# GLA value weights: differences taken by GpSimd a unit ahead from a second load, instead of by VectorE with a store and a reload

## The chip, the cores and the metric

One core of a Trainium2 chip runs the whole layer as one program. The metric is the device time in microseconds, the median of three runs; lower is better. In the text PE is TensorE (PEld its weight loads), DVE is VectorE, ACT is ScalarE, POOL is GpSimd and SP is SyncE, whose queue issues most DMAs.

## The reference

One decoder layer on 256 tokens of width 2048, in float32. Only the parts that the change touches in full:

```python
proj = x @ w_in                       # (256, 2048) @ (2048, 13336)
gq, gk, gv, gr, glr, fq, fk, fv, ff, ma, mb = jnp.split(proj, offsets, axis=-1)
# branch A: gated linear attention, 4 heads, dk 256, dv 512, diagonal decay
q = gq * DK ** -0.5; k = gk; v = gv
log_a = log_sigmoid(glr @ w_gla_lr + b_gla_lr) / TAU          # TAU = 16
o = gla_chunked(q, k, v, log_a)       # S_t = diag(a_t) S_{t-1} + k_t^T v_t, o_t = q_t S_t
o = rms_norm(o) * silu(gr); y_gla = o @ w_branch_gla
# branch B: softmax attention with forget gates, 8 heads of 128 -> y_fox
merged = sigmoid(ma) * y_gla + sigmoid(mb) * y_fox
x = layer_norm(ALPHA * x + merged @ w_out)
g = causal_dwconv(x @ w_gate); x = layer_norm(ALPHA * x + (gelu(g) * (x @ w_up)) @ w_down)
x = x + sigmoid(x @ w_ple_gate) * (p @ w_ple_proj)
```

`gv` is the product of x with a 2048 x 2048 slice of `w_in`. It is the stage that the change rebuilds.

## The kernel before

**Numbers.** Each float32 weight w is split into hi (w rounded to fp32r, by ACT, L146) and lo = w - hi (by DVE). A product is three fp32r matmuls: x_hi w_hi, x_hi w_lo, x_lo w_hi.

**Units.** All weights pass through as units of 128 x 2048 floats (1 MB), numbered in order of use. `unit()` keeps preparation three units ahead: `prep` issues the loads on SP's queue, in the order of the code, and records ACT's rounding and DVE's subtraction. `raw` (5 buffers), `hi` (6) and `lo` (6) are rings; larger tiles (8 KB a partition) come from a pool of 15 (`s8`). A scheduler orders the instructions of DVE, ACT and PE; SP's order is that of the code.

**Strassen units.** `gv`, `gr`, the output projection, the down projection and the last gate are computed by `s_half` in two column halves of 1024. In each half some of the 8 (or 22) row pairs are multiplied with seven products (`strassen`, 21 matmuls of 512 columns), the others with eight (`classic`, 24). GV is units 56 to 71, GR 72 to 87. `GV_S` names the pairs that take seven products: 11 of the 16 units. A Strassen unit holds the blocks b11, b12, b22, b21 of its weights. Its products need b11, b22, b21 and four differences, called t1 to t4: b12 - b11, b12 - b22 (together `t13`) and b22 - b11, b21 - (b22 - b11) (together `t24`). `prep_s` therefore makes four splits a unit: b11 (512 columns), b2 (1024), t13 (1024) and t24 (1024).

**Where the differences come from, before.** Eight of the 11 units are parked (`GV_T`). At a place of an earlier stage (`PARK_AT`) `park_load` loads the unit, and two places later `park_store` takes the differences on DVE (L203 for 1024 columns, L185 twice for 512) and stores them to DRAM (`td`) by a DMA from POOL's queue (L208). `prep_s` then loads b11 and b2 from the weights and reads t13 and t24 back from `td`. The other three units take their differences in `prep_s` on DVE (L185, four of 512 columns). GR's units are parked in the same way, and stay so.

**The GLA levels.** `a_gen` builds, for two pairs of heads, the decay-weighted attention inside the chunks level by level (1 to 8): DVE and ACT make exponentials and scaled q and k, PE multiplies them in fp32 (L767), and DVE copies the part under a mask into `at` (L772). Level 0 is a column sum with a matrix of ones (L728).

**The lines that the prediction names.** L146 is ACT's rounding; L185 and L203 the differences; L254 the splits in `prep_s`; L286 the split of an ordinary unit; L879 and L1012 add gv's products, and L992 a gate's, out of PSUM; L351 and L353 are matmuls of the stages ahead, L849 those of `s_half`; L341 casts the masks and L1438 copies two columns of the convolution, both on POOL; L521 is one subtraction near the start; L1061 a power on a single column, on POOL.

Of the kernel before, what the change touches and what calls it, by code (L numbers as in the profile page):

```python
# [9 lines left out]
F32 = mybir.dt.float32  # L10
# [14 lines left out]
H = 4  # L25
# [26 lines left out]
T_OG = (1, 2, 1, 1, 1, 2, 1, 1, 0, 2, 1, 1, 0, 1, 1, 3)  # L52
T_AF = (1, 1, 0, 1, 1, 1, 1, 1, 1, 1, 0, 1, 1, 1, 1, 1, 1, 0, 0, 1, 2, 1, 1, 2, 0, 2, 2, 3, 1, 1, 2, 2, 1, 1, 1, 1, 1, 1, 1, 3)
T_X2 = (2, 0, 3, 3, 1, 1)
T_MT = (2, 2, 1, 1, 0, 1, 0, 3, 0, 1, 1, 1, 1, 0, 1, 1)
WO_AT = (2, 0, 6, 1)
WO_P = (8, 0, 5)
WO_STAT = 2
DN_Z = (2, 2)
DN_AT = (3, 8, 3)  # L60
DN_P = (12, 12, 11)
XS_AT = 18
PARK_MA = (1, 5, 10)
PARK_BR = (1, 2, 7, 9)


GV_ORDER = ((1, 0, 4, 2, 3, 5, 7, 6), (1, 4, 6, 3, 2, 0, 5, 7))
GR_ORDER = ((4, 0, 3, 5, 1, 2, 7, 6), (4, 0, 6, 1, 3, 7, 2, 5))
OUT_ORDER = ((4, 5, 1, 0, 2, 3, 6, 7), (2, 0, 5, 3, 1, 6, 4, 7))
# [9 lines left out]
DN_ORDER = ((0, 1, 8, 4, 5, 3, 2, 6, 7, 9, 10, 11, 12, 15, 13, 14, 16, 17, 19, 20, 18, 21), (1, 0, 2, 5, 3, 4, 7, 9, 6, 11, 8, 15, 13, 10, 12, 14, 21, 16, 17, 19, 20, 18))  # L79
DN_S = ((1, 2, 3, 5, 7, 8, 9, 11, 13, 14, 15, 17, 19), (1, 2, 3, 5, 7, 9, 10, 11, 13, 15, 17, 19))  # L80


WO_T = ((0, 1, 2, 5), (1, 3, 5))
# [3 lines left out]
RES_N = (1, 1, 1, 4)  # L87
# [18 lines left out]
def tile_block(ctx: ExitStack, tc: tile.TileContext, wu, wfv, wpp, xT_in, x_in, pT_in, wlr,  # L106
# [48 lines left out]
    for _ in range(8):  # L155
# [17 lines left out]
              for nh in range(2) for n in tset[nh]}  # L173
    parked = {u: i for i, u in enumerate(sorted(parked))}
    td = dr.tile([len(parked), P, 2048], F32, name="td")
    sd = dr.tile([len(DN_U), P, 1024], F32, name="sd")
    hS = {}

# [19 lines left out]
    def park_store(u, w, pinned=False):  # L198
# [8 lines left out]
        differences(w[:, 0:1024], w[:, 1024:2048], 1)  # L207
        nc.gpsimd.dma_start(td[parked[u]], w)  # L208

    def park_plan(units, spots, gap=2):  # L210


        units = [u for u in parked if u in units]
        assert len(units) == len(spots), (len(units), len(spots))
        loaded = {}

        def step(n):
            for u, s in zip(units, spots):
                if s + gap == n:
                    park_store(u, loaded.pop(u), True)  # L220
            for u, s in zip(units, spots):
                if s == n:
                    loaded[u] = park_load(u)

        return step

    def prep_s(u):
# [28 lines left out]

        x11, = split(b11, "b11", slice(512, 1024))
        x22, x21 = split(r1, "b2")
        if u not in parked:
            differences(r0, r1, 0)  # L260
        t1_, t3 = split(rt[0], "t13")
        if u not in parked:
# [4 lines left out]
    def prep(pinned=False):  # L267
        u = n_prep[0]
        n_prep[0] += 1
        if u in s_units:  # L270
            prep_s(u)
            return
        his, los = [], []
        for h in range(2):
            raw = ring.tile([P, 1024], F32, tag="raw", bufs=5, name=f"raw{u}_{h}")
            nc.sync.dma_start(raw, wu[u, :, h * 1024:(h + 1) * 1024])
            hi = rhi.tile([P, 1024], F32R, tag="hi", name=f"hi{u}_{h}")
            copy(hi, raw)
# [7 lines left out]
            i = nc.vector.tensor_tensor(lo, raw, hi.bitcast(F32), ALU.subtract)  # L286
# [419 lines left out]
    at_all = at_gnb[:, 0:1536].rearrange("p (h n) -> p h n", h=H)  # L706
    gnb = at_gnb[:, 1536:2048]

    def a_gen():
        tc.keep_in_program_order(nc.gpsimd.memset(at_all, 0.0))  # L710
        for h in range(H):
            at[h] = at_all[:, h, :]
        for h in range(0, H, 2):
            hs = slice(h, h + 2)
            q, k, b = gq[:, hs, :], gk[:, hs, :], gb[:, hs, :]
# [11 lines left out]
            for i in range(2):  # L727
                nc.tensor.matmul(pa, lhsT=ones, rhs=phl[i].rearrange("p t n -> p (t n)"),  # L728
                                 start=i == 0, stop=i == 1)
            for i in range(2):  # L730
                nc.vector.copy_predicated(A[:, i, 0:256], mask[:, 0, :],
                                          pa[:, i * 256:i * 256 + 256])
            for lev in range(1, 9):
                L = 1 << lev
                h2 = L // 2
                if lev < 8:
# [17 lines left out]
                else:  # L754
                    w4 = lambda x, t: x[:, :, t * 256:t * 256 + 256].rearrange(
                        "p h (c n) -> p h c n", c=2)
                    for t, m in ((0, w4(b, 0)[:, :, :, 127:128]), (1, gt[:, hs, :, :])):
                        nc.vector.tensor_tensor(w4(e, t), w4(b, t),
                                                m.broadcast_to([P, 2, 2, P]), ALU.subtract)
                    nc.scalar.activation(e, e, AF.Exp, bias=0.0, scale=-1.0 / TAU)  # L760
                    nc.vector.tensor_tensor(km, k[:, :, 0:256], e[:, :, 0:256], ALU.mult)
                    nc.vector.tensor_tensor(qm, q[:, :, 256:512], e[:, :, 256:512], ALU.mult)
                yield
# [4 lines left out]
                                         rhs=qm[:, i, c * P:c * P + P], start=c == 0, stop=c == 1)  # L768
                pa = pa[:, 0:256].rearrange("p (h n) -> p h n", h=2)
                if lev < 8:  # L770
                    for i in range(2):
                        nc.vector.copy_predicated(  # L772
                            A[:, i, 0:256].rearrange("p (t n) -> p t n", t=2),
                            mask[:, lev, :].rearrange("p (t n) -> p t n", t=2),
                            pa[:, i:i + 1, :].broadcast_to([P, 2, P]))
                else:
                    copy(A[:, :, 256:384], pa)

# [1022 lines left out]
```

## Time and profile before

| | before |
|---|---|
| median of three runs | 1647.15 us (1645.95 to 1647.29) |
| profiled execution | 1646.94 us, its span 1644.9 us, granted clock 1.0 |
| busy, share of the span | PE 100%, DVE 82%, ACT 58%, POOL 6% |
| DMA | 470.47 MB, mean 286 GB/s |

The span runs from the first to the last instruction; about 2 us lie around it. A row of a group names line, engine, operation and tiles, then "busy us, mean ns of one | idle before it and what ended it". A row of a timeline gives start, length, then the instruction. A row of stretches gives for each engine the busy time in that stretch and the number of instructions.

### The profile page before, as it was taken

How to read it: one execution, taken by the hardware profiler on the slowest of the kernel's cores; microseconds unless marked ns; L12 is line 12 of the kernel's file. 1: busy time of each engine (PE TensorE's matmuls, PEld its weight loads, DVE VectorE, ACT ScalarE, POOL GpSimd, SP SyncE). 2: the span in 40 equal slices, each digit the busy share in tenths (PEclk: the TensorE clock that was granted, in tenths of full speed). 3: DMA queues.
4: the chain of work that ended last, by engine and by line, in shares of the span. 5: the costliest groups of instructions: out<-in, count | busy, mean ns of one | idle time of the engine just before them, and what ended most of it. 6: DMA issues, size and time to landing. Idle time of an engine off the chain costs nothing.

```text
span 1644.9 us, 23447 instructions
## 1 busy us (share of the span) xinstructions
PE 1637.0 (100%) x8407; PEld 1401.3 (85%) x8407; DVE 1355.3 (82%) x1884; ACT 946.2 (58%) x1328; POOL 104.9 (6%) x244
## 2 busy tenths in 40 slices
PE   9999999999999999999999999999999999999998
PEld 9988888888888888888898888888888888888887
DVE  7587799888988975788977888797777788988998
ACT  6654555446666664456575555555555556556655
POOL 0100000000000000000010211121111100000000
PEclk9999999999999999999999999999999999999999
DMA  8789877777877777788857889997877688999575
GB/s 325 267 297 355 295 256 257 259 272 255 323 288 275 253 270 264 272 291 318 298 192 246 283 316 350 342 365 257 277 288 287 222 299 322 348 355 339 206 267 192
DMA packets 115733, 470.47 MB, mean 286 GB/s; under 512 B 13160, under 2 KB 14448, under 8 KB 98720
## 3 DMA queue, kind: packets, MB, share of 16 engines
q1 hardware_dynamic: 106368, 413.38, 71.3%
q0 software_dynamic: 9248, 55.59, 8.4%
q8 instruction: 66, 1.08, 0.2%
q14 instruction: 51, 0.42, 0.1%
HBM read 413.33 MB, written 55.58 MB: 285 GB/s over the span
## 4 chain that ended last, share of the span: by engine, by line
PE 91%; DVE 4%; issue 2%; DMA 2%; ACT 1%; POOL 0%; ACTq 0%; SPq 0%; DVEq 0%; POOLq 0%
PE psm L974 11%; PE psu L351 10%; PE psg L351 9%; PE dn L849 7%; PE psa L974 5%; PE psu L353 5%; PE psg L353 5%; PE gr L849 3%; PE gv L849 3%; PE dn_p L849 3%; PE fv L498 3%; PE psb L974 3%; PE pg L397 2%; PE gv_p L849 2%; PE wo L849 2%
## 5 line engine op out<-in xcount | busy, mean ns | idle before, releaser
L286 DVE TENSOR_TENSOR lo<-raw,hi 128x1024 fp32r<-128x1024 f32 x450 | 546.0, 1221 | 149.3 <-ACT hi L146 147.4
L146 ACT ACTIVATE hi<-raw 128x1024 fp32r<-128x1024 f32 x450 | 473.4, 1058 | 334.1 <-PE psg L351 92.5
L351 PE MATMUL psu<-x1T,hi 128*128 128x512 f32 x688 | 240.4, 392 | 0.0
L351 PE MATMUL psg<-x1T,hi 128*128 128x512 f32 x672 | 234.8, 392 | 0.0
L353 PE MATMUL psu<-x1T,lo 128*128 128x256 f32 x688 | 192.3, 280 | 0.0
L353 PE MATMUL psg<-x1T,lo 128*128 128x256 f32 x672 | 187.8, 280 | 0.0
L974 PE MATMUL psm<-hi,xT 128*128 128x512 f32 x512 | 162.4, 391 | 0.0
L351 PEld LDWEIGHTS psu<-x1T,hi 128*128 128x128 f32 x688 | 129.2, 188 | 27.6
L351 PEld LDWEIGHTS psg<-x1T,hi 128*128 128x128 f32 x672 | 126.2, 188 | 27.0
L146 ACT ACTIVATE hi_b<-raw 128x512 fp32r<-128x512 f32 x118 | 97.9, 842 | 74.3 <-DMA raw<-in_wu_dram 24.0
L254 DVE TENSOR_TENSOR lo_b<-raw,hi_b 128x512 fp32r<-128x512 f32 x118 | 111.0, 954 | 24.6 <-ACT hi_b L146 24.4
L353 PEld LDWEIGHTS psu<-x1T,lo 128*128 128x128 f32 x688 | 130.6, 190 | 0.0
L353 PEld LDWEIGHTS psg<-x1T,lo 128*128 128x128 f32 x672 | 127.6, 190 | 0.0
L974 PEld LDWEIGHTS psm<-hi,xT 128*128 128x128 f32 x512 | 96.2, 188 | 19.6
L254 DVE TENSOR_TENSOR lo_t<-td,hi_t 128x1024 fp32r<-128x1024 f32 x82 | 97.0, 1220 | 6.7 <-ACT hi_t L146 6.5
L974 PE MATMUL psm<-lo,xT 128*128 128x512 f32 x256 | 99.7, 389 | 0.0
L146 ACT ACTIVATE hi_t<-td 128x1024 fp32r<-128x1024 f32 x82 | 84.0, 1055 | 23.2 <-DMA td<-td 11.8
L849 PE MATMUL dn<-hi,hC 128*128 128x512 f32 x304 | 84.9, 389 | 0.0
L974 PE MATMUL psa<-hi,oT 128*128 128x512 f32 x256 | 80.7, 392 | 0.0
L146 ACT ACTIVATE hi_t<-raw 128x1024 fp32r<-128x1024 f32 x36 | 38.2, 1061 | 53.4 <-DVE raw L185 46.8
L849 PEld LDWEIGHTS dn<-hi,hC 128*128 128x128 f32 x304 | 57.0, 188 | 11.8
L1438 POOL COPY gp<-gp 128x1 f32<-128x1 f32 x88 | 43.1, 522 | 276.1 <-DVE gp L380 276.1
(400 smaller groups left out, 3284.5 us busy)
## 6 DMA issues: line engine op xcount, KB each, us to landing
raw<-in_wu_dram SPq DMA_DIRECT2D x527, 512.0 KB, 5.9
td<-in_wu_dram SPq DMA_DIRECT2D x41, 1024.0 KB, 8.8
td<-td POOLq DMA_DIRECT2D x41, 1024.0 KB, 7.5
td<-td SPq DMA_DIRECT2D x41, 1024.0 KB, 8.1
hS<-sd SPq DMA_DIRECT2D x25, 512.0 KB, 7.4
raw<-in_wu_dram SPq DMA_DIRECT2D x41, 256.0 KB, 6.3
sd<-hs POOLq DMA_DIRECT2D x28, 256.0 KB, 6.2
fvraw<-in_wfv_dram SPq DMA_DIRECT2D x13, 524.0 KB, 6.6
```

The source lines that it names most:

```text
L146: return nc.scalar.activation(o, i, AF.Copy, bias=0.0, scale=scale)
L254: nc.vector.tensor_tensor(lo, src, hi.bitcast(F32), ALU.subtract)
L286: i = nc.vector.tensor_tensor(lo, raw, hi.bitcast(F32), ALU.subtract)
L351: nc.tensor.matmul(ps, lhsT=hi[i // 8 if hoff == 0 else 0][:, w0 % 1024:w0 % 1024 + P], rhs=a[:, kt % 4, :], start=first and i == 0, stop= ...
L353: nc.tensor.matmul(ps[:, 256:512], lhsT=lo[i // 8 if hoff == 0 else 0][:, w0 % 1024:w0 % 1024 + P], rhs=a[:, kt % 4, 0:256], start=False, ...
L397: nc.tensor.matmul(bs[j][:, 0:m], lhsT=x, rhs=v[:, o:o + m], start=first and i == 0, stop=last and i == 2)
L498: nc.tensor.matmul(fbk[t][c][:, 0:n], lhsT=x, rhs=w[:, o:o + n], start=kt == 0 and i == 0, stop=kt == 15 and i == 2)
L849: nc.tensor.matmul(ps, lhsT=x, rhs=w, start=todo[id(ps)] == total[id(ps)], stop=todo[id(ps)] == 1)
L974: nc.tensor.matmul(ps, lhsT=x, rhs=v, start=first and i == 0, stop=last and i == 2)
L1438: nc.gpsimd.tensor_copy(g[:, 258 + i:259 + i], g[:, 129 - i:130 - i])
```

## The change

1. `GV_T` is empty: no GV unit is parked. `PARK_AT` has the eight places of GR's units alone.
2. `near` names all 11 GV Strassen units. When `prep` comes to unit u, `near_load` is first called for u and u + 1 (`NEAR_AT = 1`), where not yet done: it loads the whole unit a second time into an `s8` tile (`nw`) on SP's queue and takes the differences in place on POOL, one subtraction of 1024 columns and two of 512. `prep_s` then loads b11 and b2 as for a parked unit and reads t13 and t24 from that tile. Nothing of it is stored.
3. In the GLA levels, level 1 is computed like level 0: a product of neighbouring q and k, one exponential, and a sum by ones in fp32r, instead of four fp32 matmuls per pair of heads. Level 8 has its reference subtracted as ACT's bias, in eight short instructions a pair instead of one long one behind two DVE subtractions. The masked copies take both heads in one instruction.
4. Tables of places and orders of other stages differ (`T_OG`, `T_MT`, `WO_AT`, `OUT_ORDER`, `WO_S`, `DN_ORDER` and others); the numbers of Strassen and parked units in those stages stay.

```diff
-PARK_AT = (1, 4, 5, 8, 13, 13, 14, 17, 22, 24, 29, 34, 37, 43, 43, 47)
+PARK_AT = (4, 8, 13, 18, 24, 32, 40, 47)
-WO_S = ((0, 1, 2, 3, 5), (1, 3, 5))
+WO_S = ((0, 1, 2, 3, 5), (0, 1, 3))
...
-GV_T = ((3, 4, 5), (2, 3, 4, 5, 6))
+GV_T = ((), ())
+NEAR_AT = 1
+GV_N = GV_S
...
+    def near_load(u):
+        w = s8([P, 2048], name=f"nw{u}")
+        nc.sync.dma_start(w, wu[u])
+        o, b, p = [w.rearrange(f, b=2, n=512) for f in (
+            "p (a b n) -> p a b n", "p (a b n) -> p b a n", "p (a b n) -> p a b n")]
+        sub = lambda o, a, b: nc.gpsimd.tensor_tensor(o, a, b, ALU.subtract)
+        sub(o[:, 0], p[:, 0, 1:2].broadcast_to([P, 2, 512]), b[:, 0])
+        b11, b12, b22, b21 = [w[:, 512 * i:512 * i + 512] for i in range(4)]
+        sub(b22, b22, b11)
+        sub(b21, b21, b22)
+        nearw[u] = w
...
-        if u in parked:
+        if u in nearw:
+            nc.sync.dma_start(b11, wu[u, :, 0:512])
+            nc.sync.dma_start(r1, wu[u, :, 1024:2048])
+            w = nearw.pop(u)
+            rt = (w[:, 0:1024], w[:, 1024:2048])
+        elif u in parked:
...
+        for v in range(u, min(NU, u + NEAR_AT + 1)):
+            if v in near and v not in near_done:
+                near_done.add(v)
+                near_load(v)
...
-            for lev in range(1, 9):
+            E, Z = ke[:, 1024:1536], ke[:, 0:512]
...
+            pa = mxtile(f"pa{h}_1")
             for i in range(2):
+                nc.tensor.matmul(pa[:, 0:256], lhsT=ones, rhs=phl[i], start=i == 0, stop=i == 1)
...
+            for lev in range(2, 9):
...
-                    nc.scalar.activation(e, e, AF.Exp, bias=0.0, scale=-1.0 / TAU)
+                    for i in range(2):
+                        for c in range(2):
+                            for t in range(2):
+                                o = t * 256 + c * P
+                                nc.scalar.activation(e[:, i, o:o + P], b[:, i, o:o + P], AF.Exp,
+                                                     bias=gref[:, t, h + i, c:c + 1],
+                                                     scale=-1.0 / TAU)
```

How this moves the instructions, at three places. The names carry the unit's number (`raw59`, `nw60`) and a buffer's; line numbers are those of each kernel. First POOL's order between the GLA levels and the first power of the attention's norm (`gst`), before:

```order
L208 DMA td_106<-td12_2922 128x2048
L208 DMA td_106<-td13_3210 128x2048
L208 DMA td_106<-td14_3212 128x2048
L208 DMA td_106<-td15_3417 128x2048
L1061 ISA
L1061 TENSOR_TENSOR gst_5281<-gst_5281,mhalf_119 128x1
```

And the same place now (the rows go on in this way to `nw70`, then `gst`):

```order
L214 DMA td_106<-td6_3026 128x2048
L214 DMA td_106<-td7_3364 128x2048
L223 ISA
L223 TENSOR_TENSOR nw56_3621<-nw56_3621 128x1024
L223 TENSOR_TENSOR nw56_3621<-nw56_3621 128x512 x2
L223 TENSOR_TENSOR nw58_3732<-nw58_3732 128x1024
L223 TENSOR_TENSOR nw58_3732<-nw58_3732 128x512 x2
L223 TENSOR_TENSOR nw59_3783<-nw59_3783 128x1024
L223 TENSOR_TENSOR nw59_3783<-nw59_3783 128x512 x2
```

POOL has lost eight stores ahead of this place and has 33 subtractions in it. Second, DVE's order at units 59 and 60 of the GV stage, before (59 was not parked, 60 was):

```order
L254 TENSOR_TENSOR lo59_b11_3878<-raw59_0_3873,hi59_b11_3877 128x512
L185 TENSOR_TENSOR raw59_0_3873<-raw59_0_3873 128x512
L185 TENSOR_TENSOR raw59_0_3873<-raw59_0_3873,raw59_1_3874 128x512
L254 TENSOR_TENSOR lo59_b2_3882<-raw59_1_3874,hi59_b2_3881 128x1024
L254 TENSOR_TENSOR lo59_t13_3888<-raw59_0_3873,hi59_t13_3887 128x1024
L185 TENSOR_TENSOR raw59_1_3874<-raw59_1_3874,raw59_0_3873 128x512
L185 TENSOR_TENSOR raw59_1_3874<-raw59_1_3874 128x512
L254 TENSOR_TENSOR lo59_t24_3894<-raw59_1_3874,hi59_t24_3893 128x1024
L254 TENSOR_TENSOR lo60_b11_3928<-raw60_0_3921,hi60_b11_3927 128x512
```

And now:

```order
L279 TENSOR_TENSOR lo59_b11_3843<-raw59_0_3838,hi59_b11_3842 128x512
L279 TENSOR_TENSOR lo59_b2_3847<-raw59_1_3839,hi59_b2_3846 128x1024
L279 TENSOR_TENSOR lo59_t13_3851<-nw59_3783,hi59_t13_3850 128x1024
L279 TENSOR_TENSOR lo59_t24_3855<-nw59_3783,hi59_t24_3854 128x1024
L279 TENSOR_TENSOR lo60_b11_3892<-raw60_0_3887,hi60_b11_3891 128x512
```

The four differences of unit 59 are gone from DVE's order; the four splits of every unit stay. Third, SP's order of loads at the same units, before:

```order
L235 DMA raw58_0_3826<-in_wu_dram 128x512
L236 DMA raw58_1_3827<-in_wu_dram 128x1024
L238 DMA td58_3830<-td_106 128x2048
L242 DMA raw59_0_3873<-in_wu_dram 128x1024
L242 DMA raw59_1_3874<-in_wu_dram 128x1024
L235 DMA raw60_0_3921<-in_wu_dram 128x512
L236 DMA raw60_1_3922<-in_wu_dram 128x1024
L238 DMA td60_3925<-td_106 128x2048
```

And now:

```order
L220 DMA nw59_3783<-in_wu_dram 128x2048
L255 DMA raw58_0_3788<-in_wu_dram 128x512
L256 DMA raw58_1_3789<-in_wu_dram 128x1024
L220 DMA nw60_3833<-in_wu_dram 128x2048
L255 DMA raw59_0_3838<-in_wu_dram 128x512
L256 DMA raw59_1_3839<-in_wu_dram 128x1024
L220 DMA nw61_3882<-in_wu_dram 128x2048
L255 DMA raw60_0_3887<-in_wu_dram 128x512
L256 DMA raw60_1_3888<-in_wu_dram 128x1024
```

The full load of a unit's differences stands one unit earlier than the reload did, ahead of the raw loads of the unit before it.

More of the change, by code (lines that the diff above doesn't have):

```diff
@@ L86 @@
 PG_ORDER = ((0, 1, 2, 3, 4, 5, 6, 7), (1, 2, 0, 3, 4, 5, 7, 6))
-RES_N = (1, 1, 1, 4)
+RES_N = (1, 1, 0, 4)
 PG_N = 5
@@ L173, in tile_block @@
               for nh in range(2) for n in tset[nh]}
+    near = {b + nh * len(order[nh]) + order[nh].index(n)
+            for b, order, tset in ((GV0, GV_ORDER, GV_N),)
+            for nh in range(2) for n in tset[nh]}
+    near_done = set()
     parked = {u: i for i, u in enumerate(sorted(parked))}
-    td = dr.tile([len(parked), P, 2048], F32, name="td")
+    td = dr.tile([max(1, len(parked)), P, 2048], F32, name="td")
     sd = dr.tile([len(DN_U), P, 1024], F32, name="sd")
@@ L258, in prep_s @@
         x22, x21 = split(r1, "b2")
-        if u not in parked:
+        if rt[0] is r0:
             differences(r0, r1, 0)
         t1_, t3 = split(rt[0], "t13")
-        if u not in parked:
+        if rt[0] is r0:
             differences(r0, r1, 1)
@@ L712, in a_gen @@
             at[h] = at_all[:, h, :]
+        b4 = gb[:, :, 0:256].rearrange("p h (c n) -> p h c n", c=2)
+        nc.vector.tensor_scalar(gref[:, 0], b4[:, :, :, 127], 1.0 / TAU, None, ALU.mult)
+        nc.vector.tensor_scalar(gref[:, 1], gt[:, :, :, 0], 1.0 / TAU, None, ALU.mult)
         for h in range(0, H, 2):
@@ L756, in a_gen @@
                         "p h (c n) -> p h c n", c=2)
-                    for t, m in ((0, w4(b, 0)[:, :, :, 127:128]), (1, gt[:, hs, :, :])):
-                        nc.vector.tensor_tensor(w4(e, t), w4(b, t),
-                                                m.broadcast_to([P, 2, 2, P]), ALU.subtract)
-                    nc.scalar.activation(e, e, AF.Exp, bias=0.0, scale=-1.0 / TAU)
+                    for i in range(2):
+                        for c in range(2):
+                            for t in range(2):
+                                o = t * 256 + c * P
+                                nc.scalar.activation(e[:, i, o:o + P], b[:, i, o:o + P], AF.Exp,
+                                                     bias=gref[:, t, h + i, c:c + 1],
+                                                     scale=-1.0 / TAU)
                     nc.vector.tensor_tensor(km, k[:, :, 0:256], e[:, :, 0:256], ALU.mult)
@@ L770, in a_gen @@
                 if lev < 8:
[L771 to L775, printed above, removed]
+                    nc.vector.copy_predicated(
+                        A[:, :, 0:256].rearrange("p h (t n) -> p h t n", t=2),
+                        mask[:, lev:lev + 1, :].rearrange("p h (t n) -> p h t n", t=2)
+                        .broadcast_to([P, 2, 2, P]),
+                        pa.unsqueeze(2).broadcast_to([P, 2, 2, P]))
                 else:
```

48 lines of the change are left out of this document (35 added, 13 removed).

## The prediction

> **What bounds the kernel now.** I read the page's engine times and its chain first, then TensorE's waits, then a table of stretches around the stage that the change rebuilds.
>
> ```profile
> PE 1637.0 (100%) x8407; PEld 1401.3 (85%) x8407; DVE 1355.3 (82%) x1884; ACT 946.2 (58%) x1328; POOL 104.9 (6%) x244
> PE 91%; DVE 4%; issue 2%; DMA 2%; ACT 1%; POOL 0%; ACTq 0%; SPq 0%; DVEq 0%; POOLq 0%
> ```
> ```profile
> PE warm_ps L156 <- DVE warm L153: 1.2, 1, 1.2
> PE dn_p L849 <- DVE lo_t L254: 0.7, 2, 0.5
> ```
>
> TensorE (PE) is busy for 1637.0 of 1644.9 us, carries 91% of the chain, and its two longest waits are 1.2 and 0.7 us. So nothing taken from another engine can win more than the 7.9 us that PE is idle, while anything that makes PE wait adds to the time at once. The question is whether the stage of the GLA values ("gv", units 56 to 71) still feeds PE. Its matmuls run at 390 to 470 us; its loads and splits begin at about 374 us.
>
> ```profile
> core 0: us, PE busy (x) PEld busy (x) DVE busy (x) ACT busy (x) POOL busy (x), PEclk, DMA share, GB/s
> 374.00:390.00 16.00, 16.00 (x73) 13.23 (x72) 15.13 (x30) 9.46 (x14) 0.00 (x0) 1.00 0.75 250
> 390.00:410.00 20.00, 20.00 (x90) 16.57 (x89) 16.47 (x18) 12.15 (x14) 0.00 (x0) 1.00 0.70 244
> 410.00:430.00 20.00, 20.00 (x90) 16.57 (x89) 19.82 (x23) 12.08 (x14) 0.00 (x0) 1.00 0.80 279
> 430.00:450.00 20.00, 20.00 (x90) 16.57 (x89) 18.76 (x21) 15.92 (x17) 0.00 (x0) 1.00 0.99 357
> 450.00:470.00 20.00, 20.00 (x90) 16.53 (x90) 16.14 (x18) 11.62 (x14) 0.00 (x0) 1.00 0.82 304
> sum 96.00, PE 96.00 PEld 79.47 DVE 86.33 ACT 61.24 POOL 0.00; mean PE 19.20 PEld 15.89 DVE 17.27 ACT 12.25 POOL 0.00
> ```
>
> In these 96 us PE never stops, VectorE (DVE) is busy for 86.33 and GpSimd (POOL) for nothing. DVE is the second engine, by a small margin; POOL looks free. How far DVE is ahead at the end of the stage, its instructions first, then PE's:
>
> ```profile
> 464.41 2.36 DVE L254 TENSOR_TENSOR lo_t<-td,hi_t 128x1024 fp32r<-128x1024 f32 x2
> ```
> ```profile
> 473.61 0.39 PE L849 MATMUL gr<-hi_t,xT 128*128 128x512 f32 x1
> ```
>
> The last split of unit 72 ends at 466.8; the product at 473.6 and the one before it (three matmuls of 0.227, so from 472.9) read it. The lead is 6.1 us. That much DVE can fall behind before PE waits.
>
> **The change, part by part.**
>
> *What DVE loses.* The edit takes the differences of units 56, 59 and 64 off DVE (L185 in this stage) and the eight parked units' differences off it earlier. The time of four lines in the same stretches, in the order L185, L879, L1012, L992 (each the sum row of its answer):
>
> ```profile
> sum 96.00, DVE 8.25; mean DVE 1.65
> ...
> sum 96.00, DVE 4.60; mean DVE 0.92
> ...
> sum 96.00, DVE 3.22; mean DVE 0.64
> ...
> sum 96.00, DVE 1.36; mean DVE 0.27
> ```
>
> DVE keeps 86.33 - 8.25 = 78.1 us. Of that 4.60 + 3.22 + 1.36 = 9.2 us read one operand from PSUM; the other 68.9 us are subtractions and sums with both operands in SBUF.
>
> *What POOL gains.* For each of 11 units one subtraction of 1024 columns and two of 512, 2048 columns in all. What matters is whether they run beside DVE's. This trace shows POOL reading SBUF while DVE does. POOL's copies of two single columns, beside DVE's splits and away from them:
>
> ```profile
> 850.28 2.25 POOL L1438 COPY gp<-gp 128x1 f32<-128x1 f32 x2 [12.14 <-DVE gp L380]
> ```
> ```profile
> 850.13 2.35 DVE L286 TENSOR_TENSOR lo<-raw,hi 128x1024 fp32r<-128x1024 f32 x2
> ```
> ```profile
> 858.07 0.30 POOL L1438 COPY gp<-gp 128x1 f32<-128x1 f32 x2 [5.54 <-DVE gp L380]
> ```
>
> The pair costs 0.30 us alone and 2.25 us beside two splits of 2.35, and ends with them (852.53 against 852.48): each copy sat out a whole DVE instruction. POOL's only wide reads say the same:
>
> ```profile
> L341 POOL CAST mask<-maskf x2: 1035/1540/2045, 44.0 to 46.0; 128x1024 uint8<-128x1024 f32 x2
> ```
> ```profile
> 43.95 1.22 DVE L521 TENSOR_TENSOR wS<-wraw,wS 16x1024 fp32r<-16x1024 f32 x1
> ```
>
> The first cast started at 44.0 beside that subtraction and took 2045 ns; the second, with none beside it, 1035 ns. The difference, 1.01 us, is about what was left of DVE's 1.22. So a POOL read and a DVE subtraction with two SBUF operands exclude each other, and fairly: POOL got in between two splits. That DVE in turn stands still while POOL reads is not in this trace (no wide POOL read starts ahead of one of its splits); I take it, since one resource that POOL must wait for whole is held by one of the two at a time.
>
> The Trainium skill's page "SBUF — State Buffer" (Summary: "The single rule") speaks against this change: a VectorE instruction with two SBUF inputs contends with a GpSimd instruction that reads SBUF, and whoever comes first holds the shared port for its whole instruction. The casts and copies agree for POOL's side; no run yet shows DVE's.
>
> *Price of POOL's subtractions.* None is in the trace. Below: one pass at the cast's 1.035 us per 1024 columns, 2.07 us a unit. Above: two passes, one for each operand, 4.14, and for each of three instructions the 556 ns that a two-operand instruction on a single column takes, 5.8 us:
>
> ```profile
> L1061 POOL TENSOR_TENSOR gst<-gst,mhalf 128x1 f32<-128x1 f32 x8 | 4.5, 556 | 219.9 <-DVE gst L1059 219.9
> ```
>
> I take 4.14 (two operands to read, and nothing shows POOL reading both at once): 11 units, 45.5 us (22.8 to 63.8). The page "GPSIMD Engine Reference" (§3.1) gives 4497 ns for 2048 columns of two operands; by it 11 units are an estimated 49.5 us, and the result below would be 4 us later.
>
> *The sum for the stage.* Time to work in: 96 + 6.1 = 102.1 us. If all of DVE's PSUM work lies beside POOL, the shared part needs 68.9 + 45.5 = 114.4, 12.3 too much; if nothing does, 78.1 + 45.5 = 123.6, 21.5 too much. I take the middle, 16.9 us of waiting on PE, since the PSUM operations stand in two clumps at the ends of the halves. With 2.07 a unit even the second sum is 100.9: no wait. With 5.8 it is 141.9: 39.8.
>
> *Transfers.* The loads per unit stay 1.75 MB where the unit was parked; three units gain 0.79 MB each.
>
> ```profile
> DMA packets 7164, 27.69 MB, mean 288 GB/s; under 512 B 800, under 2 KB 800, under 8 KB 6006
> ```
>
> 30.1 MB in 96 us is 313 GB/s, below the 357 of one stretch above: hidden by PE's work; without that cover 2.4 MB at 357 is 7 us. On SP's queue each nw load goes ahead of the raw loads of the unit before it; it may wait for a buffer, and those loads behind it, then ScalarE's and DVE's splits. In the built program four buffers take turns, and a load of this size lands in 8.2 us, so I price this at nothing. On POOL's queue the subtractions stand behind the last td store, whose differences stand ahead of unit 53's splits in DVE's new order: in time.
>
> ```profile
> td<-td SPq DMA_DIRECT2D x10, 1024.0 KB, 8.2
> ```
>
> *The new wait.* ScalarE's rounding of a unit's t13 waits for POOL's three subtractions. Queued behind it are the unit's t24 and the next unit's roundings, then DVE's splits of them, then PE. POOL starts a unit ahead, so this costs only what the sum above counts as late.
>
> *The earlier stages.* Eight loads, eight stores and eight reloads go, with 8 x (1.22 + 2 x 0.69) = 20.8 us of DVE:
>
> ```profile
> L203 DVE TENSOR_TENSOR td<-td 128x1024 f32<-128x1024 f32 x41 | 49.8, 1217 | 0.0
> L185 DVE TENSOR_TENSOR td<-td 128x512 f32<-128x512 f32 x82 | 55.9, 685 | 0.5
> ```
> ```profile
> sum 324.00, PE 323.86 PEld 281.39 DVE 264.39 ACT 176.50 POOL 11.18; mean PE 64.77 PEld 56.28 DVE 52.88 ACT 35.30 POOL 2.24
> ```
>
> From 50 to 374 us PE is busy for 323.86 of 324: DVE's relief there is worth 0.1 us at most. The smaller edits of the GLA levels (fewer DVE operations, 16 short ScalarE instructions for two long ones: ScalarE is busy 176.5 of 324) are hidden by the same PE work. The changed tables of places and orders keep the counts of units in the later stages; I price them at 0 +- 2, the size of PE's waits.
>
> *PE's own work.* Level 1 of each pair of heads loses its four fp32 matmuls (eight records) and gets two 256-column ones:
>
> ```profile
> 244.97 0.28 PE L353 MATMUL psk<-xT,lo 128*128 128x256 f32 x1
> 245.09 0.39 PE L351 MATMUL psk<-xT,hi 128*128 128x512 f32 x1
> ...
> 246.95 1.13 PE L767 MATMUL pa<-ke 128*128 128x128 f32 x8
> 247.83 0.48 PE L351 MATMUL psk<-xT,hi 128*128 128x512 f32 x1
> ```
>
> Start to start, eight records take 0.88 and one 256-column matmul 0.12: 2 x (0.88 - 0.24) = 1.3 us less.
>
> Sum against the profiled execution (1646.94, 0.2 under the median of 1647.15): 1646.9 + 16.9 - 1.3 = 1662.5 us.
>
> **Rivals.**
> 1. *The subtractions are hidden (not slower).* Place: the same stage. If 78.1 + 11 X stays below 102.1, that is if POOL takes under 2.2 us a unit (under 3.0 if all PSUM work lies beside it), or if DVE does not stand still for POOL, PE never waits: 1645.6. For it: POOL's empty row and the cast's 1035 ns for one operand; against it: the copies.
> 2. *Faster.* DVE's relief also ends PE's small waits: 1.3 and about half of the 7.9 idle us, 1641.7. Against it: those waits lie outside the stages that are relieved.
> 3. *The clock falls.* The warm-up matmuls at the start ran slower than the later ones:
>
> ```profile
> 1.19 3.59 PE warm_ps L156 x8
> ```
> ```profile
> 402.37 2.04 PE gv_p L849 x9
> ```
>
> That is 0.45 against 0.227 us each.
> ```profile
> L254 DVE TENSOR_TENSOR lo_t<-td,hi_t 128x1024 fp32r<-128x1024 f32 x82 | 97.0, 1220 | 6.7 <-ACT hi_t L146 6.5
> ...
> L254 DVE TENSOR_TENSOR lo_b<-raw,hi_b 128x512 fp32r<-128x512 f32 x59 | 40.5, 686 | 7.5 <-ACT hi_b L146 7.4
> ```
>
> A Strassen unit of 21 matmuls would take 9.4 us instead of 4.76, against about 8.2 that DVE and POOL in turn need for one (3 x 1.22 + 0.69 less some overlap of DVE's, and 4.14): 1.2 us more for each of 11 units, 13 us: 1675.7. The page "TensorE: Matmul & The Clock Gate" (Part 1) has the clock halved after about 3.4 us idle; a single POOL instruction would hold PE for less. The granted clock is 1.00 in every stretch above, so no row shows it behind a gap.
>
> **How the numbers follow.** About 0.2% (3.3 us) is what a measurement of this kernel can tell from no change. Chances: forecast 0.74, hidden 0.13, faster 0.05, clock 0.08. Slower is the first and the last, 0.82; same 0.13; faster 0.05. The forecast's own range is 1652 to 1676 (12.3 less 4 for a start before 374 us; 21.5 plus some order lost). The range given, 1645 to 1682, takes in the hidden case and most of the clock's; the ends at 5.8 us a unit (1685) and at 1642 stay out.
>
> **What would show it.** In the changed profile: POOL busy for 45 us or more between 374 and 490; its 1024-column subtractions at 2 us or longer; DVE's splits in that stage with a mean well above 1.22; PE with 12 to 22 us of waits for DVE lo in gv matmuls, and none of size elsewhere; 324 us up to 374 unchanged but for 1.3. The prediction is wrong if DVE's splits keep 1.22 us beside POOL's subtractions, or if these take under 1.1 us for 1024 columns.

## The result and the profile after

The changed kernel takes 1665.07 us (median of 4 runs, 1663.96 to 1668.10), the kernel before 1646.63 beside it (median of 4): 1.0116 times the time, 95% interval 1.0104 to 1.0128. The forecast was 1662.5 (1645 to 1682). The profiled execution took 1663.96 us, its span 1662.2.

The page's engine times, after; then PE's three longest waits, which stood at 1.2 us and less before:

```profile
PE 1643.4 (99%) x8395; PEld 1402.1 (84%) x8395; DVE 1368.8 (82%) x1831; ACT 949.4 (57%) x1342; POOL 173.9 (10%) x268
```
```profile
PE gv_p L912 <- DVE lo_t L279: 6.6, 5, 2.3
PE gv L912 <- DVE lo_b L279: 3.7, 4, 2.3
PE gv_p L912 <- DVE lo_b L279: 1.6, 3, 0.8
```

DVE's total has risen by 13.5 us with 53 instructions fewer, and all of PE's new waits of size are for DVE's splits in gv (line 279, 254 before). The same stretches as in the prediction, and the sum row of the 324 us ahead of them:

```profile
374.00:390.00 16.00, 16.00 (x72) 13.26 (x71) 15.68 (x17) 8.28 (x13) 11.89 (x7) 1.00 0.86 335
390.00:410.00 20.00, 17.65 (x71) 13.94 (x70) 19.75 (x15) 10.24 (x12) 11.14 (x5) 0.91 0.52 184
410.00:430.00 20.00, 19.83 (x86) 15.73 (x85) 19.73 (x18) 11.54 (x14) 12.19 (x6) 1.00 0.79 300
430.00:450.00 20.00, 13.76 (x53) 9.51 (x52) 20.00 (x12) 9.17 (x10) 19.53 (x10) 0.96 0.56 212
450.00:470.00 20.00, 16.82 (x57) 11.47 (x56) 20.00 (x12) 10.32 (x11) 13.88 (x6) 0.87 0.44 150
sum 96.00, PE 84.06 PEld 63.92 DVE 95.16 ACT 49.56 POOL 68.63; mean PE 16.81 PEld 12.78 DVE 19.03 ACT 9.91 POOL 13.73
...
sum 324.00, PE 323.86 PEld 281.24 DVE 250.99 ACT 180.77 POOL 13.43; mean PE 323.86 PEld 281.24 DVE 250.99 ACT 180.77 POOL 13.43
```

Ahead of the stage DVE is busy for 13.4 us less (20.8 was the forecast for the differences alone), and PE gains nothing from it, as forecast. In the stage DVE is now "busy" for 95.16 of 96 us, with 74 instructions instead of 110. Busy here includes standing still. The tile `nw` (duration as least/median/most), then two of DVE's groups by shape:

```profile
L223 POOL TENSOR_TENSOR nw<-nw x33: 1297/2158/6050, 365.2 to 465.7; 128x512 f32<-128x512 f32 x22, 128x1024 f32<-128x1024 f32 x11
```
```profile
L279 DVE TENSOR_TENSOR lo_t<-nw,hi_t 128x1024 fp32r<-128x1024 f32 x22 | 41.1, 1908 | 0.0
...
L1075 DVE TENSOR_TENSOR vg<-vg,gv 128x512 f32<-128x512 f32 x6 | 3.7, 675 | 0.0
```

The same split took 1220 ns before. The sum that reads one operand from PSUM kept its 675. One subtraction of POOL lasted 6.05 us, beside three splits of DVE in a row and the start of a fourth:

```profile
419.96 6.05 POOL L223 TENSOR_TENSOR nw<-nw 128x1024 f32<-128x1024 f32 x1 [7.58 <-DMA nw<-in_wu_dram]
...
420.27 3.48 DVE L315 TENSOR_TENSOR lo<-raw,hi 128x1024 fp32r<-128x1024 f32 x3
```

PE's clock: the matmul behind one of its two longest gaps, then the stretch that holds the gap and the slow one behind it, and the two other slow stretches (the column behind POOL's is the granted clock):

```profile
393.44 0.50 PE L912 MATMUL gv_p<-lo_t,xS 128*128 128x512 f32 x1 [2.35 <-DVE lo_t L279]
```

```profile
390.50:393.80 3.30, 0.95 (x5) 0.48 (x4) 3.30 (x2) 1.37 (x2) 3.22 (x2) 1.00 0.00 0
393.90:397.20 3.30, 3.30 (x10) 2.39 (x9) 3.30 (x3) 1.06 (x1) 2.76 (x2) 0.50 0.00 0
...
448.50:451.80 3.30, 2.91 (x7) 2.09 (x8) 3.30 (x3) 1.12 (x2) 3.30 (x2) 0.50 0.19 63
...
458.80:462.00 3.20, 3.20 (x9) 2.55 (x8) 3.20 (x4) 0.63 (x1) 1.09 (x1) 0.50 0.92 344
```

The gap itself cost 2.35 us, and the next 3.3 us ran at half speed. The account of the 17.3 us between the spans, from the distances of PE's matmuls from start to start (a working over all of them, not a row): 14.2 us of gaps and 6.3 us of matmuls that took longer than usual between 370 and 500 us, 0.5 of small change there, 1.3 less work, and 2.4 less lost in the other stages. Of the 6.3 us at most 5.1 are the clock's: it stood at 0.50 for three stretches of 3.4 us. The rest are matmuls right behind a gap, which follow each other after 0.34 us instead of 0.227 while the granted clock is 1.00.

### The profile page after: what moved, and what is told of

Same layout as the page of the kernel before. It is cut to its first block, busy times and chain, and to the rows that moved or that the text cites. A ratio compares the mean times of both kernels' runs of the same rounds, so it can differ in the third digit from the quotient of the medians.

```text
span 1662.2 us, 23416 instructions
## 1 busy us (share of the span) xinstructions
PE 1643.4 (99%) x8395; PEld 1402.1 (84%) x8395; DVE 1368.8 (82%) x1831; ACT 949.4 (57%) x1342; POOL 173.9 (10%) x268
## 4 chain that ended last, share of the span: by engine, by line
PE 90%; DVE 5%; issue 3%; DMA 1%; ACT 1%; POOL 0%; SPq 0%; DVEq 0%; ACTq 0%; POOLq 0%
PE psu L380 9%; PE psg L380 9%; PE psm L1037 9%; PE dn L912 9%; PE psa L1037 5%; PE psu L382 5%; PE psg L382 5%; PE dn_p L912 4%; PE wo L912 3%; PE gr L912 3%; PE fv L527 3%; PE pg L426 2%; PE psb L1037 2%; PE psk L380 2%; PE psq L380 2%
## 5 line engine op out<-in xcount | busy, mean ns | idle before, releaser
L279 DVE TENSOR_TENSOR lo_b<-raw,hi_b 128x512 fp32r<-128x512 f32 x118 | 122.4, 1053 | 18.0 <-ACT hi_b L148 17.8
L279 DVE TENSOR_TENSOR lo_t<-td,hi_t 128x1024 fp32r<-128x1024 f32 x64 | 75.5, 1217 | 3.9 <-ACT hi_t L148 3.8
L223 POOL TENSOR_TENSOR nw<-nw 128x512 f32<-128x512 f32 (+1 forms) x33 | 75.1, 2283 | 30.9 <-DMA nw<-in_wu_dram 14.6
L148 ACT ACTIVATE hi_t<-td 128x1024 fp32r<-128x1024 f32 x64 | 65.6, 1054 | 13.0 <-DMA td<-td 4.6
L912 PEld LDWEIGHTS dn<-hi,hC 128*128 128x128 f32 x304 | 57.0, 188 | 12.3
```

The lines of the kernel that those rows point to most:

```text
L148: return nc.scalar.activation(o, i, AF.Copy, bias=0.0, scale=scale)
L223: sub = lambda o, a, b: nc.gpsimd.tensor_tensor(o, a, b, ALU.subtract)
L279: nc.vector.tensor_tensor(lo, src, hi.bitcast(F32), ALU.subtract)
L912: nc.tensor.matmul(ps, lhsT=x, rhs=w, start=todo[id(ps)] == total[id(ps)], stop=todo[id(ps)] == 1)
```

## The experiments

Theory: POOL's subtractions and DVE's subtractions both read SBUF and exclude each other, so DVE loses the time of one POOL instruction after another, and PE waits for DVE. Rivals: the differences come late, and ScalarE's rounding with everything behind it waits; the second loads crowd the DMA queues; POOL's writes are in the way.

### Is it POOL's work, its lateness, or its loads?

First, POOL subtracts as before, and the splits read the raw block:

```diff
-            w = nearw.pop(u)
-            rt = (w[:, 0:1024], w[:, 1024:2048])
+            nearw.pop(u)
+            rt = (r1, r1)
```

> The changed kernel, with POOL's 33 subtractions kept where they are but read by nobody: t13 and t24 are split from the plain blocks b22, b21 that are in SBUF anyway (so the differences are left out of the values). Theory 1, shared reads: POOL and DVE exclude each other whatever becomes of POOL's result, so the stage stays slow: 1657 to 1666, DVE's splits beside POOL at 1.8 us mean or more. Rival, late results: the loss is ScalarE and PE waiting for POOL's differences, which nothing waits for now: 1641 to 1646, splits at 1.22.

Second to fourth, with that edit, the three subtractions give way to nothing, to three fills that only write, and to five copies with one operand:

```diff
-        sub(o[:, 0], p[:, 0, 1:2].broadcast_to([P, 2, 512]), b[:, 0])
-        sub(b22, b22, b11)
-        sub(b21, b21, b22)
+        for _ in range(3): nc.gpsimd.memset(w[:, 0:1792], 0.0)              # third
+        for _ in range(5): nc.gpsimd.tensor_copy(w[:, 0:1024], w[:, 1024:2048])  # fourth
```

> As the run with unread subtractions, and POOL's 33 subtractions left out; the second loads of 1 MB a unit stay. Theory 1: nothing else was slow, 1641 to 1646, a little below the kernel before (1.3 us less PE work, and about 2.5 us fewer PE stalls after 500 us that the new tables brought). Rival, transfers: the second loads and their place in SP's queue cost the time: 1655 or more.

> As the run with unread subtractions, but POOL only writes in their place: three fills of 1792 columns into the same tile, about 4.9 us a unit. Theory 1 in its narrow form, only POOL's reads exclude DVE's second operand: 1641 to 1646, splits at 1.22 us. Wide form, any POOL instruction on SBUF holds DVE up: 1657 to 1666, as with the subtractions.

> As the run with unread subtractions, but POOL copies in their place: five copies of 1024 columns, one operand each, about 5.2 us a unit. Theory 1: a read of one operand excludes DVE as one of two does, and what counts is POOL's time: 1657 to 1668. Rival, only POOL instructions with two operands collide: 1641 to 1646.

All four leave the differences out of the values.

| beside before at 1646.04 | time | ratio (95%) |
|---|---|---|
| subtractions that nobody reads | 1666.83 | 1.0125 (1.0110 to 1.0140) |
| no POOL work, second loads kept | 1644.95 | 0.9992 (0.9983 to 1.0002) |
| fills | 1644.64 | 0.9992 (0.9983 to 1.0001) |
| copies | 1660.79 | 1.0089 (1.0074 to 1.0104) |

DVE's split of the upper blocks with unread subtractions, then the sum row of the 96 us without POOL work; then the fills' group and sum row; then the copies' group and the split beside them:

```profile
L279 DVE TENSOR_TENSOR lo_t<-raw,hi_t 128x1024 fp32r<-128x1024 f32 x22 | 41.1, 1908 | 0.0
```
```profile
sum 96.00, PE 96.00 PEld 79.23 DVE 76.33 ACT 59.41 POOL 0.00; mean PE 19.20 PEld 15.85 DVE 15.27 ACT 11.88 POOL 0.00
```
```profile
L224 POOL MEMSET nw<- x33: 1595/1600/1608, 365.6 to 449.7; 128x1792 f32 x33
...
sum 96.00, PE 96.00 PEld 79.25 DVE 76.48 ACT 59.27 POOL 47.82; mean PE 19.20 PEld 15.85 DVE 15.30 ACT 11.85 POOL 9.56
```
```profile
L224 POOL COPY nw<-nw x55: 1044/1914/2487, 365.6 to 471.4; 128x1024 f32<-128x1024 f32 x55
...
L276 DVE TENSOR_TENSOR lo_t<-raw,hi_t 128x1024 fp32r<-128x1024 f32 x22 | 38.8, 1800 | 0.0
```

With subtractions that nobody waits for, the split still has a mean of 1908 ns and the time is that of the changed kernel (0.8 us above the upper end of what was expected): lateness of the differences is out. Without POOL's work all is gone, second loads and all: the transfers cost nothing. 47.8 us of POOL fills change neither DVE's sum (76.48 against 76.33) nor PE's: writes are not in the way. One-operand reads are: beside the copies the split takes 1800 ns.

### The price, measured alone

One kernel with these instructions only, executed once:

```diff
+    stage((pool_unit, 3))                                     # the three subtractions of a unit
+    stage((split, 6), (shorts, 6), (psum_op, 6), (one, 6))    # DVE's kinds, alone
+    stage((split, 14), (pool_unit, 5))                        # then each beside POOL
+    stage((shorts, 60), (pool_unit, 5))
+    stage((psum_op, 40), (pool_unit, 5))
+    stage((one, 40), (pool_unit, 5))
+    for cols in (64, 512, 768, 1024, 1280, 1536, 2048, 2560): hole(cols)   # PE's gaps
```

> A kernel that leaves out the whole layer and only times instructions, in stretches between barriers: POOL's three subtractions of a unit, three times, alone; DVE's split of 1024 columns, its sum of 128, its sum of 512 with one PSUM operand and its copy of 512, each alone; then each of the four in a long row on DVE beside five units of subtractions on POOL; then matmuls in rows of 120 with holes of different length between them. Theory (POOL's subtractions and DVE's two-operand instructions in SBUF exclude each other, one whole instruction at a time): a unit takes POOL 5.0 us alone (2.45 and twice 1.3); beside splits and beside sums of 128 columns each DVE instruction is followed by one POOL instruction, so 14 splits beside 15 subtractions end after about 14 x 1.22 + 25 = 42 us, and the first 15 of 60 sums take 25 us longer than alone (each 0.28 us long, each waiting 1.3 to 2.4); beside the PSUM sums and the one-operand copies both engines keep their times. Rival (both only share a rate): every instruction of both gets longer in proportion, sums of 128 columns wait 0.3 us or less each. Holes: if gaps of about 2.3 us halve the clock, the granted clock falls for about 3.4 us behind every hole of that length and longer, and not behind those of 1 us; if only gaps of about 3.4 us do, only behind the longest.

POOL's two sizes alone, by group; then the timeline of the stages, POOL alone, DVE alone, and the pairs:

```profile
L136 POOL TENSOR_TENSOR nw<-nw 128x512 f32<-128x512 f32 x6 | 7.6, 1262 | 0.5
L136 POOL TENSOR_TENSOR nw<-nw 128x1024 f32<-128x1024 f32 x3 | 7.0, 2338 | 8.5 <-SPq L159 8.5
```

```profile
8.93 14.97 POOL L136 TENSOR_TENSOR nw<-nw 128x1024 f32<-128x1024 f32 x9 [8.48 <-SPq L159]
...
23.97 7.52 DVE L144 TENSOR_TENSOR lo<-raw,hi 128x1024 fp32r<-128x1024 f32 x6 [21.45 <-SPq L159]
31.41 1.92 DVE L148 TENSOR_TENSOR sums<-sums,xy 128x128 f32<-128x128 f32 x6
33.36 4.32 DVE L152 TENSOR_TENSOR sums<-quiet,xy 128x512 f32<-128x512 f32 x6
37.72 2.73 DVE L156 COPY sums<-xy 128x512 f32<-128x512 f32 x6
...
40.53 35.23 DVE L144 TENSOR_TENSOR lo<-raw,hi 128x1024 fp32r<-128x1024 f32 x14
...
78.34 25.22 POOL L136 TENSOR_TENSOR nw<-nw 128x1024 f32<-128x1024 f32 x15
...
78.30 25.41 DVE L148 TENSOR_TENSOR sums<-sums,xy 128x128 f32<-128x128 f32 x16 [2.54 <-SPq L159]
...
118.18 25.01 POOL L136 TENSOR_TENSOR nw<-nw 128x1024 f32<-128x1024 f32 x15 [14.62 <-SPq L159]
...
118.20 28.97 DVE L152 TENSOR_TENSOR sums<-quiet,xy 128x512 f32<-128x512 f32 x40
147.30 38.06 DVE L156 COPY sums<-xy 128x512 f32<-128x512 f32 x40
```

A unit takes POOL 14.97 / 3 = 4.99 us alone. Beside splits the two take turns, one whole instruction each: 14 splits took 35.23 us instead of 14 x 1.25 = 17.5, 17.7 more for 13 of POOL's subtractions, 4.1 a unit. Beside sums of 128 columns POOL ran on at its own pace (25.2 for five units) and DVE got one sum in for each subtraction: 16 sums took 25.4 us instead of 5.1, again 4.1 a unit (POOL's whole 5.0 was expected). Of 60 such sums the first 16 paid for everything. The sum with a PSUM operand took 28.97 for 40, 28.8 by its time alone, and POOL 25.0: neither noticed the other. The copy, one operand in SBUF, lost 38.06 - 18.2 = 19.9 us, 4.0 a unit; that was a miss, since I had expected it to be free.

So the price in the sum, what DVE loses for a unit, is 4.0 to 4.1 us. The changed kernel bears it out: between 374 and 490 us DVE's instructions with two SBUF operands took 38.0 us more than at their length before, beside ten units of POOL's, 3.8 a unit (a sum over the groups of both traces, not a row). DVE needs 1.22 + 2 x 0.69 = 2.6 us to do the same subtractions itself. The work moved to POOL costs DVE more than keeping it.

For PE the kernel leaves gaps of different length between rows of 120 matmuls. The rows that follow the last three gaps, with the idle time ahead, and the stretches behind the gaps:

```profile
359.98 27.52 PE L171 MATMUL acc<-act,wt 128*128 128x512 f32 x120 [2.24 <-DVE act L180]
390.46 30.37 PE L171 MATMUL acc<-act,wt 128*128 128x512 f32 x120 [2.96 <-DVE act L180]
424.52 5.73 PE L171 MATMUL acc<-act,wt 128*128 128x512 f32 x18 [3.68 <-DVE act L180]
```
```profile
357.50:361.50 4.00, 1.76 (x9) 1.25 (x8) 2.08 (x3) 0.00 (x0) 0.00 (x0) 1.00 0.02 4
390.40:396.60 6.20, 6.14 (x14) 4.81 (x15) 0.00 (x1) 0.00 (x0) 0.00 (x0) 0.50 0.01 3
424.50:427.30 2.80, 2.78 (x7) 2.21 (x8) 0.00 (x0) 0.00 (x0) 0.00 (x0) 0.50 0.00 0
```

Gaps up to 2.24 us left the clock at 1.00 here, those of 2.96 and 3.68 halved it; 6.2 us at half speed followed the middle one, 2.8 the longer one. Three groups of short gaps at the end of the kernel (four of 0.52 us, four and two of 0.79) left it at 1.00. In the changed kernel a gap of 2.35 was enough.

### How much of it the stage can carry

The other edits alone, gv parked as before; the same with POOL taking the three units that were not parked; and all 33 subtractions on DVE instead of POOL:

```diff
-GV_N = GV_S
+GV_N = ((), ())            # p1; PARK_AT and GV_T as before the change
+GV_N = ((1, 2), (1,))      # p2; the same
-        sub = lambda o, a, b: nc.gpsimd.tensor_tensor(o, a, b, ALU.subtract)
+        sub = lambda o, a, b: nc.vector.tensor_tensor(o, a, b, ALU.subtract)   # p4
```

> The changed kernel with GV's eight units parked again at the places of before and the other three on DVE; no second loads, nothing on POOL. It is the other edits alone. Theory 1: they save 1.3 us of PE work and about 2.5 us of PE stalls behind 500 us: 1641 to 1645. Rival, the tables cost as much as they give: 1645 to 1648.

> The changed kernel with GV's eight units parked again and POOL taking the differences of the three others alone (56, 59, 64). Shared part by the sum of the prediction with POOL at 5.0 us a unit: 68.9 + 15 = 84 us, with all of DVE 78.1 + 15 = 93, both below 102.1: no wait of PE, 1641 to 1645, the same as with the eight parked and three on DVE. Rival, each POOL subtraction delays PE wherever it stands: 1.6 us a unit of the 17 lost by 11, so 1646 to 1650.

> The changed kernel with the 33 subtractions of the second loads on DVE instead of POOL. DVE then needs 78.1 + 11 x (1.22 + 2 x 0.69) = 106.7 us less some overlap of its own, against 102.1: 0 to 5 us of waiting over 1643, so 1643 to 1649, faster than on POOL by 15 us or more, since POOL's read holds DVE for longer than DVE would need. Rival, the loads a unit ahead are late: as slow as the change, 1660 or more.

Then POOL for the first half of gv alone, the second parked as before, and the other way round; and the first half, and all of gv, with POOL two units ahead:

```diff
-GV_N = GV_S
+GV_N = (GV_S[0], ())       # p3, p5; GV_T and PARK_AT park the other half
+GV_N = ((), GV_S[1])       # p7; the same
-NEAR_AT = 1
+NEAR_AT = 2                # p5, p6
```

> The changed kernel with the first half of GV as changed (five units on POOL) and the second half as before (five units parked, unit 64 on DVE). Sum of the prediction with POOL at 5.0 us a unit: shared part 68.9 + 25 + 2.75 = 97, all of DVE 106, against 102.1: 0 to 4 us of waiting, 1643 to 1649. Rival, in proportion to units: 5 of 11 of about 20 us, 9 us over 1643: 1651 to 1654.

> p3_half with its loads and POOL's subtractions two units ahead instead of one (NEAR_AT = 2). In p3_half POOL's first subtraction began at 374.4 us, in the changed kernel at 365.2, and the second Strassen unit's split then came 6.3 us late. Theory 1 (the half has too little time because POOL started late, its total of shared work is not too much): starting a unit earlier takes the waits away, 1643 to 1648 us. Theory 2 (each DVE instruction behind which POOL has work waits out one subtraction, and the crowd of short sums stands there whatever the start): the waits stay at 5 us or more, 1652 to 1658.

> The changed kernel with NEAR_AT = 2. Theory (too much shared work for the stage, with a lead that is spent once): one more unit of lead is worth at most the 5 to 8 us of one unit once, 1656 to 1662 us. Rival: the tile buffers are full and the loads wait for them, so nothing starts earlier, 1663 to 1668.

> The first half of gv as before (three units parked, two taking their differences on DVE), the six Strassen units of the second half on POOL: p3_half turned round. In p1_park_back DVE is busy for 43.3 us between 422 and 470; without L191's 2.8 and with 7.8 us of PSUM work beside POOL 32.7 us are left that exclude POOL's reads, and six units at the 4.99 us that a unit takes alone are 29.9. Theory A (the sum holds for each half by itself, with these prices): 62.7 against 48 + 6.1, or 57.7 if POOL does one unit ahead, so 3.6 to 8.6 us of waiting and up to 3 more from the clock, 1648 to 1656 us. Theory B (a half is only dear where a crowd of short DVE sums stands in it, each of which waits out a whole subtraction; they stand ahead of 395 us alone): the second half has none of them, 1644 to 1648.

| kernel | time | before beside it | ratio (95%) |
|---|---|---|---|
| p1: other edits alone | 1644.68 | 1646.77 | 0.9991 (0.9982 to 1.0000) |
| p2: three units on POOL | 1644.58 | 1646.77 | 0.9987 (0.9978 to 0.9995) |
| p4: subtractions on DVE | 1651.79 | 1646.77 | 1.0033 (1.0022 to 1.0044) |
| p3: first half on POOL | 1657.18 | 1646.77 | 1.0064 (1.0051 to 1.0078) |
| p5: the same, two units ahead | 1661.23 | 1646.97 | 1.0086 (1.0071 to 1.0101) |
| p6: all, two units ahead | 1669.94 | 1646.97 | 1.0140 (1.0123 to 1.0157) |
| p7: second half on POOL | 1659.65 | 1647.24 | 1.0076 (1.0059 to 1.0092) |

p1 shows the other edits as a small gain: the medians differ by 2.1 us, and the interval is 0 to 3.0. p2 adds three units that lie apart from each other (56, 60 and 64 in the changed order of units; its text says 59) and costs nothing; it is the fastest kernel here, but its gain over p1 (0.1 us) is none that can be told. p4 is slower than expected by 3 us, and still 13 us faster than with POOL: DVE's 78.1 us and 11 x 2.6 make 106.7 against the 102.1 of the prediction, 4.6 too much, and PE's gaps come to 5.5.

p3 was the clear miss. I had let half the load share the time of the whole stage. Its chain at the start of gv, DVE's instructions:

```profile
387.46 1.37 DVE L868 TENSOR_TENSOR sums<-xy,sums 128x128 f32<-128x128 f32 x1
388.76 0.41 DVE L1004 TENSOR_TENSOR xS<-sums,xS 128x256 fp32r<-128x256 f32 x1
389.09 1.38 DVE L868 TENSOR_TENSOR sums<-xy 128x128 f32<-128x128 f32 x1
390.40 2.62 DVE L1004 TENSOR_TENSOR xS<-sums,xS 128x256 fp32r<-128x256 f32 x1
...
394.21 0.28 DVE L868 TENSOR_TENSOR sums<-sums,xy 128x128 f32<-128x128 f32 x1
...
395.68 3.37 DVE L279 TENSOR_TENSOR lo_t<-nw,hi_t 128x1024 fp32r<-128x1024 f32 x1
```
```profile
390.00:410.00 20.00, 11.49 (x37) 8.40 (x36) 19.92 (x17) 7.08 (x10) 11.29 (x7) 0.74 0.37 129
```

A sum of 0.28 us takes 1.37 when POOL has a subtraction under way, one of 0.41 takes 2.62. Behind this crowd stands the last split (t24) of the first Strassen unit, 56, and PE waits 6.3 us for it (the text on p5 calls it the second unit's); the clock falls to 0.74 over the stretch. p5 tested whether POOL had only begun too late: its first subtraction moved from 374.4 to 366.8 us.

```profile
366.79 6.34 POOL L223 TENSOR_TENSOR nw<-nw 128x1024 f32<-128x1024 f32 x3 [3.01 <-DMA nw<-in_wu_dram]
```
```profile
PE gv L912 <- DVE sb L1055: 6.9, 1, 6.9
```

It did not help: the longest wait moved to another short DVE instruction, and 1661 us is above both expectations. p6 says the same of the whole stage, where I had expected a gain or at most no change. So an earlier start of POOL did not help in either. p7 has no such crowd, and was not cheap either, 4 us above the upper end that I had given:

```profile
422.00:470.00 48.00, 39.06 (x147) 28.55 (x146) 47.24 (x31) 24.10 (x26) 35.83 (x16) 0.93 0.61 222
```

What fits the second half is the rate in a run of Strassen units. DVE's splits of one take 3 x 1.22 + 0.69 = 4.35 us, with 4.05 for POOL's turns 8.4, and PE uses it up in 21 x 0.227 = 4.77: 3.6 us lost a unit. The second half has five in a row (1, 4, 3, 6, 2), 18.2 less the lead of 6.1 makes 12.1; in p7 PE's gaps are 11.0, and of the 14.2 in the changed kernel 11.3 lie in the second half. Slow matmuls add 4.1 in p7, of which the clock can be 3.4 (0.07 of 48 us). The classic units behind a run have time to spare, but it comes too late for that run. This fits two kernels and was not tested by one of its own.

The first half only seems to fit. It has four in a row (4, 3, 2, 5), 14.5 less 6.1 makes 8.4, and PE's gaps in p3 are 8.8. But they lie elsewhere; PE's row behind the long one, and a later stretch, in p3:

```profile
399.11 0.80 PE L912 MATMUL gv_p<-lo_t,xS 128*128 128x512 f32 x1 [6.30 <-DVE lo_t L279]
```
```profile
410.00:430.00 20.00, 20.00 (x90) 16.49 (x89) 17.52 (x15) 15.45 (x17) 6.73 (x3) 1.00 0.65 219
```

All 8.8 us are lost inside the first Strassen unit, before the run of four begins at 411.3, and PE goes through that run without a gap. So 8.4 against 8.8 is chance: by its place, what cost time in p3 is the crowd of short sums, which p7 doesn't have. Why POOL's earlier start made p5 and p6 slower still (gaps 13.0 and 18.9), while the changed kernel with a start at 365.2 lost only 2.9 in its first half, stays open; DVE's order changes with the start.

## Why the prediction was right, and where not

- *PE bounds the kernel, DVE has 6.1 us of lead.* Right: all new waits are in gv and for DVE's splits, and PE is busy for 323.86 of the 324 us ahead of it, as before.
- *DVE keeps 78.1 us without the differences.* Right: 76.3 in the kernel without POOL work.
- *Reads exclude each other, in both directions.* DVE's side, which was taken without a row, is shown: splits of 1908 ns with a least of 1210, and 1908 again where nobody reads the result. The Trainium skill's page "SBUF — State Buffer" ("Who interferes with whom" and the Summary) says that the one that comes second blocks until the first is done, and that GpSimd instructions that only write stay out of it; the turns in the small kernel and the fills agree.
- *PSUM work lies beside POOL freely.* Right as a mechanism: 28.97 us against 28.8.
- *4.14 us a unit, from two passes of a cast.* As what DVE loses it was right, 4.0 to 4.1, but by luck: it was meant as POOL's own time, which is 4.99, and about 0.3 us of each instruction does not hold DVE up ((4.99 - 4.05) / 3).
- *16.9 us of waiting.* The listed waits are 11.9, PE's gaps 14.2, inside 12.3 to 21.5. The term that was left out of the forecast is the clock: up to 5.1 of the 6.3 us of slow matmuls.
- *One sum for the whole stage.* This is the weak step. The same sum gave 0 to 4 us for p3, where the gaps were 8.8, and taken by halves 3.6 to 8.6 for p7, where they were 11.0. That it came close for all 11 units together is in part luck: by their places the waits hang on where POOL's work meets a crowd of short sums or a run of Strassen units, and the sum sees neither. The upper end of the forecast's own range, 1676, also holds some 9 us that the prediction doesn't work out (1645.6 + 21.5 is 1667).
- *Rival 3, the clock falls.* Given 0.08 and 13 us, it happened in part, about 5 us. The step that failed is the argument that "a single POOL instruction would hold PE for less" than the idle time that halves the clock: a gap of 2.35 us was enough. The Trainium skill's page "TensorE: Matmul & The Clock Gate" (Part 1) speaks of an idle window of about 3.4 us that runs freely; the slow stretches of 3.4 us fit that length, the gap of 2.35 was shorter than the page asks, and the measurement decides.
- *PE's own work -1.3, tables 0 +- 2.* p1 gives -2.1 for both by the medians (0 to -3.0), so the tables' share can't be told from nothing. They don't keep every count: the output projection parks six units instead of seven (`WO_T`), and gv's and gr's own orders differ too. In the sum, 16.9 became 14.2 + 6.3 + 0.5, and the other stages gave 2.4 back: the mechanism was right, one term was missing, and part of it was cancelled. That 1662.5 lies so near the profiled 1663.96 is luck.
- *The signs named.* POOL busy for 68.6 us (45 or more), its subtractions of 1024 columns 2.34 us alone (2 or more), splits at 1908 ns: all there, and no wait of size outside gv.
- *Transfers and the queues: nothing.* Right: with the loads and without POOL's work 0.9992.
- *Rivals 1 and 2.* Refuted for 11 units. Rival 1 holds for three units apart from each other (p2).

## What to carry to other kernels

Before work is moved from VectorE to GpSimd, ask whether both read SBUF: here most GpSimd instructions held up one VectorE instruction for most of their own length, and a unit cost VectorE 4.05 us moved away against 2.6 us kept. What can go beside it is work that only writes, or VectorE work with an operand in PSUM. A sum over a whole stage is a bound only if work can be carried through it; look for runs of dense units and for crowds of short VectorE instructions in it, and add the clock once TensorE's gaps add up to some 1.6 us or more in 3.4 (the section below).

## What the hardware showed that was not expected

Turns are not always taken: the subtraction of 6.05 us above needs 2.34 alone, and DVE ran three splits ahead of it. A short DVE instruction pays as much as a long one, 0.28 us becoming 1.37. A copy on DVE with a single SBUF operand collides too, 0.43 us alone and 1.74 beside POOL in the small kernel:

```profile
L156 DVE COPY sums<-xy 128x512 f32<-128x512 f32 x15 | 26.0, 1736 | 0.6
```

And gaps far below 3 us can halve the clock: of a gap of 2.24 us in the small kernel and one of 2.35 in the changed kernel, the second did and the first did not. The traces' record of the granted clock shows what sets them apart (a working over ten traces, not rows: the changed kernel, p1, p3 to p7, the unread subtractions, the copies and the small kernel). Each slow stretch within the stages lasts 3.41 us or two or three times that: three of 3.41 in the changed kernel, one of 6.83 in p7, one of 10.24 in p3. The stretches at 1.00 between them are whole multiples as well, 51.2 and 6.83 us in the changed kernel. So the clock is set on a beat of 3.41 us. A beat at full speed in which PE was idle for 1.98 us or more was always followed by a slow one, one with 1.61 or less never; between these both happened. The gap of 2.35 us lay inside one beat, that of 2.24 was cut by the border of two, 1.36 and 0.88. The two later slow stretches of the changed kernel stood behind several shorter gaps, 1.98 and 1.64 us of idle time in one beat. The ends of matmuls are modelled, so these bounds are rough, and no run was made to test them.
